# Routed experts offset by a pair: gate/up, a block of full-array products, then down of the preceding pair

## The chip, the cores and the metric

One core of a Trainium2 chip. The metric is the device time of one execution in microseconds (us). PE is TensorE, DVE is VectorE, ACT is ScalarE, POOL is GpSimd; SP is SyncE, whose queue issues the loads of the weights.

## What is computed

A network for 256 tokens of width 1024: two layers of a mixer and a routed feed-forward part with layer norms, and then two layers of three modulated sub-blocks each. The change lies in the routed experts of the first two layers:

```python
def routed_moe(x, router_w, router_b, w_gate, w_up, w_down):
    ...
    gates = ...          # for each token 2 of 16 experts, weights that sum to 1
    y = jnp.zeros_like(xt)
    for e in range(N_EXPERTS):
        h = jax.nn.silu(xt @ w_gate[e]) * (xt @ w_up[e])
        y = y + gates[:, e:e + 1] * (h @ w_down[e])
    return y.reshape(B, S, D)

ffn = routed_moe(x, ...)
x = layer_norm(ALPHA * x + ffn, ln_g[l, 1], ln_b[l, 1])
```

The inner width of an expert is 512, all of it in float32.

## The kernel before, in words

The program is a sequence of phases A to J. `in_weights` holds the weights of all phases in the order in which they are used, as loads of 1 MB, each of two chunks of 128 x 1024 numbers. SP issues the loads into a ring of blocks of 8 KB per partition (`NBLK = 23`, shared with the activations), as early as the plan of the blocks allows (`schedule`, `pump`, `raw`, L501). What the engines do is written as a program of tiles; a scheduler puts the instructions of each engine in order, so that a product which waits for something can stand behind later ones that are ready. All products go through `mm` (L587) and all transposes through `tr` (L591). An f32 product shows as two instructions of PE in the trace, one of type f32r as one.

Phases B and D (`phase_moe`, one for each of the first two layers) are the routed experts. Each expert takes its tokens in 64 slots. Two experts make a pair, eight pairs a phase, and the weights of a pair are 24 chunks: 16 of gate and up, 8 of down. `expert_pair` does for one pair:

- gate/up: per k-tile and expert two products of 64 columns with 512 numbers out, into `pg` and `pu`, one expert in the upper half of the partitions, the other in the lower half; 32 products. Then silu (ACT, L1352) and the product with up (DVE, L1353) make h.
- four transposes of h, copied by ACT (L1358) as hT.
- down: 16 products of 64 columns into two banks y; they leave y with the gate's factor and in two parts of type f32r, by ACT (L1379) and DVE (L1380).
- combine: eight products of all 128 columns with the transposed one-hot PT bring the slots back to the tokens; four additions into x by DVE (L1387).

Every second pair the slots of the next four experts are made: `onehot` (DVE, L1283), `gather` (32 products of 128 x 256, which leave by ACT, L1305, and DVE, L1302), and `slots` (transposes of the one-hots, and products that give the gates of the slots). After pair 5 `overflow` asks if an expert has more than 64 tokens: a branch on all engines (L1413, L1414). Its body does not run with these inputs. After it `gain_rows` makes sixteen transposes for the layer norm that follows. The last pair's combine goes into banks that hold x already, by products with the identity, and the layer norm takes it from there.

`behind` is a way to say that what is issued in it stands behind a given instruction in the order of its engine.

Of the kernel before, what the change touches and what calls it, by code (L numbers as in the profile page):

```python
# [18 lines left out]
D = 1024  # L19
# [7 lines left out]
# ---------------------------------------------------------------- host layout  # L27
# [27 lines left out]
# how many of the modulation's 144 columns of chunks are done by the end of a phase  # L55
# [13 lines left out]
def _mix_plan(p):  # L69
    """how many of its modulation chunks follow each of the main chunks of a phase"""  # L70
# [53 lines left out]
def _moe(inp, l):  # L124
    g, u, d = inp['moe_w_gate'][l], inp['moe_w_up'][l], inp['moe_w_down'][l]
    out = []
    for e in range(0, NE, 2):
# [149 lines left out]
def _consts():  # L277
# [18 lines left out]
    # of the attentions alone  # L296
# [44 lines left out]
class Null:  # L341
    """stands for any part of a program while its memory is planned"""
# [41 lines left out]
NW0, NW2 = 5, 2  # L384
# [3 lines left out]
class Net:  # L388
    NBLK = 23

    def __init__(self, ctx, tc, aps, phases, plan=None):
# [14 lines left out]
        self.nsplit, self.phase, self.last_mm = 0, None, []  # L406
# [5 lines left out]
    # ---- memory: blocks of 8 KB, for activations and for the weights that run ahead  # L412
# [19 lines left out]
    def free_up(self, u, lag):  # L432
        """the block is likely free `lag` weight chunks from now"""
# [8 lines left out]
    def schedule(self):  # L442
        """the event after which each weight load may be issued: as early as the blocks allow"""
# [45 lines left out]
    # ---- weight stream  # L489
# [57 lines left out]
    def splits_behind(self, *ins):  # L547
        """the next splits queue behind these instructions"""
# [12 lines left out]
    def behind(self, *ins):  # L561
        """what is issued here queues behind these instructions, each on its engine"""
# [6 lines left out]
    def sooner(self, n):  # L569
        """what is issued here goes before what came up to n instructions earlier, where either could"""  # L570
# [13 lines left out]
    # ---- matrix products  # L584

    def mm(self, out, a, b, start=True, stop=True):
        self.last_mm = [self.nc.tensor.matmul(out, lhsT=a, rhs=b, start=start, stop=stop)]  # L587
        return self.last_mm[0]

    def tr(self, out, a):  # L590
        self.nc.tensor.transpose(out, a, self.ident)  # L591
# [18 lines left out]
    def row(self, acc, x, first, last):  # L610
        """token-major product of one [128, 1024] slab; x = (hi, lo) [128, 256]"""
# [9 lines left out]
    def tail(self, acc, items, fin):  # L621
        """the last slabs of a token-major product, a piece of the output at a time; fin(t, n) follows piece n"""
# [13 lines left out]
    def hilo(self, src, hi, lo, eng=None):  # L636
        """exact parts of a tensor"""
# [3 lines left out]
    def feat_parts(self, x, t, scale, bias, hi, lo, act=False):  # L641
        """x [128 tok, 1024] of token tile t: x * scale + bias, feature-major, in parts"""
# [25 lines left out]
    def everywhere(self, a):  # L668
        """a vector of 1024, read once per partition"""
# [15 lines left out]
    # ---- constants  # L685

    def setup(self):
# [43 lines left out]
        self.onesb = cst.tile([128, 128], BF, name="onesb")  # L731
# [10 lines left out]
        self.modc = cst.tile([128, 2, 3, 24], F32, name="modc")  # L742
# [19 lines left out]
    def constants(self, *names):  # L762
        """a block with constants that only one phase needs"""
# [5 lines left out]
    # ---- norms  # L769
# [1540 lines left out]
```

## Time and profile before

| | |
|---|---|
| runs | 1987.99, 1991.94, 1994.36 us; median 1991.94 |
| the profiled execution | span 1988.0 us |
| PE | 95% busy, 11556 instructions |
| DVE | 60% |
| ACT | 44% |
| POOL | 24% |
| read from HBM | 504.00 MB, 254 GB/s over the span |
| granted clock of PE | 0.9 or more in each of 40 slices |

The span is that of the profiled execution, on the only core in use. PE's share over the span is a mean over phases with different limits, so the phases B and D are read by themselves: B from about 140 to 389 us, D from about 529 to 778 us. The granted clock 1.00 is 2.4 GHz, 0.50 is 1.2 GHz.

### The profile page before, as it was taken

Reading aid. Unit: us, or ns where it says so; the run is one execution under the profiler, and the core shown is the slowest. Engines: PE = TensorE matmul, PEld = TensorE weight load, DVE = VectorE, ACT = ScalarE, POOL = GpSimd, SP = SyncE. Lnnn points to the kernel's source line nnn. Section 1 sums busy time; section 2 is a strip of 40 time slices with the busy share of each in tenths; the row PEclk is TensorE's granted clock in tenths of the full one; section 3 lists DMA queues with packets and bytes.
Section 4 is the critical chain, followed back from the end, with each engine's and each line's share of the span. In section 5 each row is a group of like instructions: output and inputs, shape, how many; then the busy total and the mean of one; then the engine's idle time right before and its main releaser. Section 6 shows DMA issues by size and latency. Waiting matters only on the chain.

```text
span 1988.0 us, 29007 instructions
## 1 busy us (share of the span) xinstructions
PE 1885.5 (95%) x11556; PEld 1475.4 (74%) x11556; DVE 1186.6 (60%) x1951; ACT 878.2 (44%) x1522; POOL 475.8 (24%) x300
## 2 busy tenths in 40 slices
PE   7999998889999988999999899999989999999998
PEld 7874443377644434899898779998989888878997
DVE  6752221388421214989689978765977684567453
ACT  6631111166321112444597645455434566656443
POOL 2100000141000002343343332222431322354232
PEclk9999999999999999999999999999999999999999
DMA  9569999546799995787424558756786444555520
GB/s 388 208 242 358 406 421 371 217 151 232 296 354 419 421 387 238 299 336 275 180 90 176 210 213 317 299 189 249 277 336 236 170 149 147 193 212 212 195 103 33
DMA packets 70982, 507.08 MB, mean 255 GB/s; under 512 B 7856, under 2 KB 8112, under 8 KB 10032
## 3 DMA queue, kind: packets, MB, share of 16 engines
q1 hardware_dynamic: 70256, 503.15, 64.6%
q8 instruction: 94, 1.54, 0.3%
q10 hardware_dynamic: 576, 1.93, 0.2%
q14 instruction: 56, 0.46, 0.1%
HBM read 504.00 MB, written 1.05 MB: 254 GB/s over the span
## 4 chain that ended last, share of the span: by engine, by line
PE 47%; DVE 7%; ACT 4%; POOL 3%; issue 3%; DMA 0%; DVEq 0%; POOLq 0%; ACTq 0%
PE ph L587 27%; PE pg L587 19%; DVE t L580 2%; PE ph L591 1%; DVE t L539 1%; ACT t L579 1%; POOL t L580 1%; DMA t<-in_weights 0%; POOL w L2181 0%; ACT ph L844 0%; POOL t L2018 0%; DVE w L936 0%; DVE t L639 0%; DVE t L938 0%; POOL t L639 0%
## 5 line engine op out<-in xcount | busy, mean ns | idle before, releaser
L587 PE MATMUL pg<-t,t 128*128 128x512 f32 (+4 forms) x4702 | 974.1, 404 | 25.7 <-POOL t L580 9.1
L587 PEld LDWEIGHTS pg<-t,t 128*128 128x128 f32 (+1 forms) x4702 | 668.5, 180 | 244.6 <-issue 136.4
L587 PE MATMUL ph<-t,t 128*128 128x256 f32 (+3 forms) x4550 | 592.5, 290 | 7.1 <-ACT t L1615 3.1
L587 PEld LDWEIGHTS ph<-t,t 128*128 128x128 f32 (+2 forms) x4550 | 564.9, 192 | 25.0 <-ACT t L1615 4.1
L580 POOL TENSOR_TENSOR t<-t,t 128x1024 fp32r<-128x1024 f32 (+2 forms) x122 | 319.9, 2626 | 918.4 <-ACT t L579 809.3
L579 ACT ACTIVATE t<-t 128x1024 fp32r<-128x1024 f32 (+4 forms) x414 | 425.6, 1049 | 255.7 <-DVE t L580 60.6
L580 DVE TENSOR_TENSOR t<-t,t 128x1024 fp32r<-128x1024 f32 (+1 forms) x292 | 413.9, 1430 | 123.4 <-ACT t L579 120.8
L539 DVE SCALAR_TENSOR_TENSOR t<-t,cact 128x1024 f32<-128x1024 f32 x144 | 202.6, 1419 | 32.7 <-DMA t<-in_weights 32.5
L587 PE MATMUL ph<-t,w 128*64 128x512 f32 (+3 forms) x712 | 172.9, 546 | 7.6 <-ACT w L1358 6.0
L587 PEld LDWEIGHTS ph<-t,w 128*64 128x64 f32 (+1 forms) x712 | 70.4, 146 | 106.5 <-issue 71.4
L1353 DVE TENSOR_TENSOR w<-w,pg 128x512 f32<-128x512 f32 x16 | 11.0, 688 | 173.0 <-PE pg L587 129.4
L1380 DVE SCALAR_TENSOR_TENSOR t<-ph,rgsl,t 128x512 fp32r<-128x512 f32 x32 | 23.1, 748 | 150.1 <-ACT t L1379 149.9
L1352 ACT ACTIVATE w<-pg 128x512 f32<-128x512 f32 x16 | 9.6, 597 | 200.8 <-PE pg L587 200.8
L639 DVE TENSOR_TENSOR t<-w,t 128x256 fp32r<-128x256 f32 x96 | 79.9, 832 | 21.3 <-ACT t L638 21.2
L638 ACT ACTIVATE t<-w 128x256 fp32r<-128x256 f32 x107 | 43.6, 409 | 97.1 <-DVE w L1756 84.8
L1379 ACT ACTIVATE t<-ph,rgsl 128x512 fp32r<-128x512 f32 x32 | 20.9, 685 | 121.8 <-PE ph L587 121.3
L1756 DVE TENSOR_TENSOR w<-w,ph 128x256 f32<-128x256 f32 x88 | 36.6, 416 | 52.4 <-PE ph L587 50.6
L591 PE MATMUL ph<-kc,t 128*128 128x128 f32 x248 | 39.2, 284 | 25.0 <-DVE t L890 11.0
L1552 POOL MEMSET t<- 64x256 f32 x2 | 0.6, 306 | 250.8 <-PEq L1414 191.3
L1755 ACT ACTIVATE w<-ph 128x256 f32<-128x256 f32 x88 | 32.8, 372 | 51.3 <-PE ph L587 44.5
L587 PEld LDWEIGHTS ph<-w,t 128*128 128x128 f32 (+1 forms) x384 | 40.5, 171 | 18.1 <-issue 11.9
L591 PEld LDWEIGHTS ph<-kc,t 128*128 128x128 f32 x248 | 28.3, 143 | 33.8 <-issue 16.1
(334 smaller groups left out, 1408.8 us busy)
## 6 DMA issues: line engine op xcount, KB each, us to landing
t<-in_weights SPq DMA_DIRECT2D x475, 1024.0 KB, 7.5
t<-in_xT SPq DMA_DIRECT2D x2, 512.0 KB, 5.1
t<-in_weights SPq DMA_DIRECT2D x2, 512.0 KB, 6.5
t<-in_x SPq DMA_DIRECT2D x1, 1024.0 KB, 13.3
t<-in_gate_cols ACTq DMA_DIRECT2D x1, 864.0 KB, 7.0
t<-in_consts_attn SPq DMA_DIRECT2D x1, 512.0 KB, 3.5
t<-in_final_g ACTq DMA_DIRECT2D x1, 512.0 KB, 3.3
out<-t SPq DMA_DIRECT2D x2, 256.0 KB, 2.0
```

The costliest lines, as they stand in the source:

```text
L539: self.nc.vector.scalar_tensor_tensor(w, w, 1.0, self.cact, op0=OP.mult, op1=OP.mult, accum_out=acc)
L579: self.nc.scalar.activation(t[:, 0, :n], w[:, :n], AF.Copy)
L580: eng.tensor_tensor(t[:, 1, :n], w[:, :n], t[:, 0, :n].bitcast(F32), op=OP.subtract)
L587: self.last_mm = [self.nc.tensor.matmul(out, lhsT=a, rhs=b, start=start, stop=stop)]
L591: self.nc.tensor.transpose(out, a, self.ident)
L638: self.nc.scalar.activation(hi, src, AF.Copy)
L639: (eng or self.nc.vector).tensor_tensor(lo, src, hi.bitcast(F32), op=OP.subtract)
L1353: v.tensor_tensor(h, h, pu, op=OP.mult)
L1379: self.evac = nc.scalar.activation(yy[:, 0, ns], y[n], AF.Copy, scale=gsl[:, pr, :])
L1380: v.scalar_tensor_tensor(yy[:, 1, ns], y[n], gsl[:, pr, :], yy[:, 0, ns].bitcast(F32), op0=OP.mult, op1=OP.subtract)
L1755: nc.scalar.activation(a, g, AF.Silu)
L1756: nc.vector.tensor_tensor(a, a, u, op=OP.mult)
```

## The change

The pairs are offset by one. Step s does gate/up of pair s, then a block of the full-array products that are ready (the transposes of pair s - 1, gather and slots of the next four experts, combine of pair s - 2), then down of pair s - 1. The stream of weights has that order too. `pinned` puts each of the three behind the last instruction that PE was given, so that the scheduler doesn't mix them. The branch of the overflow stands after gate/up of pair 5, `gain_rows` in the block of step 6. Around it `NW0` (buffers of small tiles) goes from 5 to 6, the modulation's columns are changed in place and `modc` is gone, a matrix of ones becomes a column that is broadcast, a statistics tile shrinks, and comments are removed. In the changed kernel the lines are: `mm` L596, `tr` L601, silu L1359, its product L1360, hT L1368, y leaves by L1387 (ACT) and L1388 (DVE), additions into x L1413, the branch L1420 and L1421.

```diff
 def _moe(inp, l):
...
+    def gate_up(e):
...
+    def down(e):
...
+    gate_up(0)
+    for e in range(2, NE, 2):
+        gate_up(e)
+        down(e - 2)
+    down(NE - 2)
     return out
...
-NW0, NW2 = 5, 2
+NW0, NW2 = 6, 2
...
     def mm(self, out, a, b, start=True, stop=True):
         self.last_mm = [self.nc.tensor.matmul(out, lhsT=a, rhs=b, start=start, stop=stop)]
+        self.last_pe = self.last_mm[0]
         return self.last_mm[0]
...
-        def expert_pair(pr, xg, PT, gsl, nextw, fin=None, step=None, slots=None):
+        def gate_up(pr, xg, nextw, h, step=None):
...
-            PT = PT or slots()
-            h = self.w2([128, 512])
             nc.scalar.activation(h, pg, AF.Silu)
             v.tensor_tensor(h, h, pu, op=OP.mult)
+            return h
+
+        def turn(h, hT):
...
+        def down(pr, hT, gsl, nextw, then):
...
-            def combine(n):
+            def leave(n):
                 ns = PIECES[0][n]
                 self.evac = nc.scalar.activation(yy[:, 0, ns], y[n], AF.Copy, scale=gsl[:, pr, :])
                 v.scalar_tensor_tensor(yy[:, 1, ns], y[n], gsl[:, pr, :], yy[:, 0, ns].bitcast(F32),
                                        op0=OP.mult, op1=OP.subtract)
...
+                then(n, yy)
...
+        def combine(pr, yy, PT, n, c=None):
...
+        def pinned():
+
+            return self.behind(*[self.last_pe] * (self.last_pe is not None))
...
-        for p2 in range(4):
-            for pr in (2 * p2, 2 * p2 + 1):
-                PT = expert_pair(pr, cur[0][1], cur[1], gsl, stream, last if pr == 7 else None, None if pr else step,
-                                 lambda: slots(0, P, gsl, new))
-                cur = cur[0], PT
-                if pr % 2 == 0 and p2 < 3:
-                    nxt = pick(p2 + 1)
-            if p2 == 2:
-                overflow(cur[0])
...
+        for s in range(8):
+            p2 = s // 2
+            if s % 2 and p2 < 3:
+                P = onehot(p2 + 1, new)
+            with pinned():
+                hs[s] = gate_up(s, xg, stream, self.w2([128, 512]), None if s else step)
+            if s == 5:
+                overflow((ug, xg))
+                self.last_pe = None
+            if s % 2:
+                self.release(ug)
+            with pinned():
+                if s:
+                    hT = turn(hs.pop(s - 1), self.w2([128, 4, 128]))
+                else:
+                    PT[0] = slots(0, P, gsl, new)
+                if s % 2 and p2 < 3:
+                    ug, xg, _ = gather(P)
+                    PT[p2 + 1] = slots(p2 + 1, P, gsl, new)
+                if s == 5:
+                    self.release(*us)
+                if s > 1:
+                    uy, yy = ys.pop(s - 2)
+                    for n in range(2):
+                        combine(s - 2, yy, PT[s // 2 - 1], n)
+                    self.release(uy)
+                if s == 6:
+                    self.gb = self.gain_rows(l, 1)
...
+            if s:
+                with pinned():
+                    ys[s - 1] = down(s - 1, hT, gsl, stream, later)
...
+        with pinned():
+            h = hs.pop(7)
+            hT = turn(h, self.w2([128, 4, 128]))
+            c = {}
+            for t in range(2):
+                for n, ns in enumerate(PIECES[t]):
+                    c[t, n] = self.pg()
+                    self.mm(c[t, n], self.ident, x[:, t, ns], True, False)
+            uy, yy = ys.pop(6)
+            for n in range(2):
+                combine(6, yy, PT[3], n, c)
+            self.release(uy)
+        with pinned():
+            uy, _ = down(7, hT, gsl, stream, lambda n, yy: combine(7, yy, PT[3], n, c))
```

The order on PE before, in phase B around the end of a pair's down: `ph` with 64 rows is y of down, `ph` with 128 rows is combine, `pg` is gate/up of the next pair (one row is one product).

```order
L587 MATMUL ph_2124<-t_1956,w_393_2121 64x512
L587 MATMUL ph_2125<-t_1956,w_393_2121 64x512
L587 MATMUL pg_2174<-t_1956,t_1996 64x512
L587 MATMUL ph_2152<-t_2123,w_315_1771 128x512
L587 MATMUL ph_2156<-t_2123,w_315_1771 128x512
L587 MATMUL pg_2175<-t_1956,t_1996 64x512
L587 MATMUL ph_2152<-t_2123,w_315_1771 128x512
L587 MATMUL ph_2156<-t_2123,w_315_1771 128x512
L587 MATMUL ph_2162<-t_2123,w_315_1771 128x512 x2
L587 MATMUL ph_2166<-t_2123,w_315_1771 128x512 x2
L587 MATMUL pg_2174<-t_1962,t_1996 64x512
```

The same place on PE with the change: the end of gate/up, the block of a step of an even number (four transposes, combine), and the begin of down.

```order
L596 MATMUL pg_2102<-t_1960,t_1985 64x512
L596 MATMUL pg_2103<-t_1960,t_1985 64x512
L601 MATMUL ph_2155<-kc,w_350_1925 128x128 x4
L596 MATMUL ph_2161<-t_2070,w_312_1766 128x512 x2
L596 MATMUL ph_2165<-t_2070,w_312_1766 128x512 x2
L596 MATMUL ph_2169<-t_2070,w_312_1766 128x512 x2
L596 MATMUL ph_2173<-t_2070,w_312_1766 128x512 x2
L596 MATMUL ph_2178<-t_1960,w_400_2154 64x512
L596 MATMUL ph_2179<-t_1960,w_400_2154 64x512
L596 MATMUL ph_2178<-t_1966,w_400_2154 64x512
```

Combine now stands as one piece between the two runs of 64-column products, and its y is that of the pair before the one whose h is turned ahead of it.

The order on DVE before, in phase B for one pair: the product of silu and up (L1353), the second half of y's two pieces (L1380), the four additions into x (L1387).

```order
L1353 TENSOR_TENSOR w_391_2113<-w_391_2113,pg_2066 128x512
L1380 SCALAR_TENSOR_TENSOR t_2123<-ph_2124,rgsl_1510,t_2123 128x512
L1380 SCALAR_TENSOR_TENSOR t_2123<-ph_2125,rgsl_1510,t_2123 128x512
L1387 TENSOR_TENSOR t_67<-t_67,ph_2152 128x512
L1387 TENSOR_TENSOR t_67<-t_67,ph_2156 128x512
L1387 TENSOR_TENSOR t_67<-t_67,ph_2162 128x512
L1387 TENSOR_TENSOR t_67<-t_67,ph_2166 128x512
```

The same on DVE with the change, in a step of an even number.

```order
L1360 TENSOR_TENSOR w_389_2101<-w_389_2101,pg_2103 128x512
L1413 TENSOR_TENSOR t_67<-t_67,ph_2161 128x512
L1413 TENSOR_TENSOR t_67<-t_67,ph_2165 128x512
L1413 TENSOR_TENSOR t_67<-t_67,ph_2169 128x512
L1413 TENSOR_TENSOR t_67<-t_67,ph_2173 128x512
L1388 SCALAR_TENSOR_TENSOR t_2177<-ph_2178,rgsl_1509,t_2177 128x512
L1388 SCALAR_TENSOR_TENSOR t_2177<-ph_2179,rgsl_1509,t_2177 128x512
```

The additions of one pair now stand directly behind the product of silu and up of a later pair, and ahead of the evacuation of y of the pair between them.

## Rows read from the trace of the kernel before

**Rows 1.** The head of the page: span and instructions.

```profile
span 1988.0 us, 29007 instructions
```

**Rows 2.** Windows: busy time of each engine (instructions), PE's granted clock, DMA share, GB/s.

```profile
core 0: us, PE busy (x) PEld busy (x) DVE busy (x) ACT busy (x) POOL busy (x), PEclk, DMA share, GB/s
139.60:388.70 249.10, 235.98 (x1049) 101.95 (x1049) 50.68 (x96) 36.82 (x64) 1.62 (x5) 0.99 0.89 361
205.00:313.00 108.00, 103.21 (x476) 44.90 (x476) 22.87 (x44) 14.73 (x26) 0.00 (x0) 1.00 1.01 418
324.30:331.00 6.70, 5.93 (x22) 4.07 (x24) 0.00 (x0) 2.39 (x4) 0.61 (x2) 0.50 0.67 230
```

**Rows 3.** Waits of PE in B, 139 to 389 us: total, times, longest.

```profile
PE ph L591 <- DVE w L1353: 4.7, 5, 1.4
PE ph L591 <- DVEq L1414: 3.7, 1, 3.7
PE ph L587 <- ACT w L1358: 3.0, 4, 0.7
PE pg L587 <- ACT t L1379: 0.8, 1, 0.8
PE ph L587 <- ACT t L1379: 0.8, 1, 0.8
```

**Rows 4.** Waits of SP in the same stretch, its largest group.

```profile
SPq L501 <- PE ph L587: 75.7, 29, 6.6
```

**Rows 5.** DMA issues from 205 to 313 us: count, KB each, median us to landing.

```profile
t<-in_weights SPq DMA_DIRECT2D x45, 1024.0 KB, 15.9
```

**Rows 6.** Timeline of PE, 149 to 179 us: start, duration, instruction, count.

```profile
149.67 7.14 PE L587 MATMUL pg<-t,t 128*64 128x512 f32 x32
156.74 0.44 PE L591 MATMUL ph<-kc,w 128*128 128x128 f32 x2
...
158.08 1.07 PE L587 MATMUL pg<-t,t 128*64 128x512 f32 x2
159.08 0.66 PE L591 MATMUL ph<-kc,w 128*128 128x128 f32 x4
...
170.98 1.66 PE L587 MATMUL ph<-t,w 128*128 128x512 f32 x6
172.48 1.12 PE L587 MATMUL ph<-w,t 128*128 128x256 f32 x8
173.52 1.93 PE L587 MATMUL pg<-t,t 128*64 128x512 f32 x6
175.38 3.07 PE L587 MATMUL ph<-w,t 128*128 128x256 f32 x24
178.30 0.38 PE L591 MATMUL ph<-kc,w 128*128 128x128 f32 x2
```

**Rows 7.** Timeline of PE's weight loads in one run: first and last of 13.

```profile
194.49 0.15 PEld L587 LDWEIGHTS ph<-t,w 128*64 128x64 f32 x2 [0.28 <-issue]
...
199.64 0.15 PEld L587 LDWEIGHTS ph<-t,w 128*64 128x64 f32 x2 [0.28 <-issue]
```

**Rows 8.** Timeline of PE: behind the overflow's branch, and products by the identity.

```profile
325.07 3.65 PE L591 MATMUL ph<-kc,cols 128*128 128x128 f32 x16 [3.75 <-DVEq L1414]
...
359.64 1.98 PE L587 MATMUL pg<-t,kc 128*128 128x512 f32 x4
```

**Rows 9.** Timeline of PE: last down and end of B; begin and end of D.

```profile
376.08 4.51 PE L587 MATMUL ph<-t,w 128*64 128x512 f32 x18
...
388.69 2.35 PE L591 MATMUL ph<-kc 128*128 128x128 f32 x20
...
547.41 1.07 PE L587 MATMUL pg<-t,t 128*64 128x512 f32 x2
...
777.85 5.62 PE L591 MATMUL ph<-kc 128*128 128x128 f32 x50
```

**Rows 10.** The additions into x on DVE, over the span: shortest/median/longest ns.

```profile
L1387 DVE TENSOR_TENSOR t<-t,ph x56: 679/682/690, 171.5 to 747.7; 128x512 f32<-128x512 f32 x56
```

More of the change, by code (lines that the diff above doesn't have):

```diff
@@ L774, in normed @@
         nc, v = self.nc, self.nc.vector
-        st = self.small("lnst", [128, 2, 3, 6])
+        st = self.small("lnst", [128, 2, 2, 6])
         mv = self.small("lnmv", [128, 2, 2])
@@ L855, in prep @@
         v = self.nc.vector
-        c = self.modc[:, l, s, :]
-        v.tensor_tensor(c[:, :16], self.mod[:, l, s, :16], self.col(f'ab{l}{s}', 0, 16), op=OP.add)
+        c = self.mod[:, l, s, :]
+        v.tensor_tensor(c[:, :16], c[:, :16], self.col(f'ab{l}{s}', 0, 16), op=OP.add)
         v.scalar_tensor_tensor(c[:, 8:16], c[:, 8:16], 1.0, self.col(f'ng{l}{s}', 0, 8), op0=OP.add, op1=OP.mult)
@@ L862, in prep_gate @@
         v = self.nc.vector
-        c = self.modc[:, l, s, 16:]
-        v.tensor_tensor(c, self.mod[:, l, s, 16:], self.col(f'ab{l}{s}', 16, 8), op=OP.add)
+        c = self.mod[:, l, s, 16:]
+        v.tensor_tensor(c, c, self.col(f'ab{l}{s}', 16, 8), op=OP.add)
         v.tensor_scalar(c, c, 1.0, 1.0 if s == 1 else 0.5, op0=OP.add, op1=OP.mult)
@@ L873, in enter @@
         ul, lo = self.alloc([128, 8, S], F32R)
-        c = self.modc[:, l, s, :]
+        c = self.mod[:, l, s, :]
         uxs, xs = self.alloc([128, 2, 1024])
@@ L1356, in expert_pair, with some @@
                 self.tr(pt[:, k, :], h[:, k * 128:(k + 1) * 128])
-            hT = self.w2([128, 4, 128])
             nc.scalar.activation(hT, pt, AF.Copy)
+            return hT
+        def down(pr, hT, gsl, nextw, then):
             uy, yy = self.alloc([128, 2, 1024], F32R)
-            c = {}
-            if fin:
-                for t in range(2):
-                    for n, ns in enumerate(PIECES[t]):
-                        c[t, n] = self.pg()
-                        self.mm(c[t, n], self.ident, x[:, t, ns], True, False)
             y = [self.ph(), self.ph()]
-            def down(parts):
+            def some(parts):
                 for s in range(2):
@@ L1381, in combine @@
                                        op0=OP.mult, op1=OP.subtract)
-                for t in range(2):
-                    o = c[t, n] if fin else self.ph()
-                    for j in range(2):
-                        self.mm(o, PT[pr % 2][:, t * 128:(t + 1) * 128], yy[:, j, ns], j == 0 and not fin, j == 1)
-                    if not fin:
-                        v.tensor_tensor(x[:, t, ns], x[:, t, ns], o, op=OP.add)
+                then(n, yy)
             if pr == 7:
                 for n in range(2):
-                    down(((n, 0), (n, 1)))
-                    down(((n, 2), (n, 3)))
-                    combine(n)
+                    some(((n, 0), (n, 1)))
+                    some(((n, 2), (n, 3)))
+                    leave(n)
             else:
                 for k in range(4):
-                    down(((0, k), (1, k)))
+                    some(((0, k), (1, k)))
                 for n in range(2):
-                    combine(n)
-            fin_ = fin(h) if fin else None
-            for t, n in c:
-                with self.sooner(TAIL_AHEAD):
-                    fin_(t, n, c[t, n])
-            if fin:
-                self.release(self.gb[0])
-            self.release(uy)
-            return PT
+                    leave(n)
+            return uy, yy
+        def combine(pr, yy, PT, n, c=None):
+            ns = PIECES[0][n]
+            for t in range(2):
+                o = c[t, n] if c else self.ph()
+                for j in range(2):
+                    self.mm(o, PT[pr % 2][:, t * 128:(t + 1) * 128], yy[:, j, ns], j == 0 and not c,
+                            j == 1 and (pr == 7 or not c))
+                if not c:
+                    v.tensor_tensor(x[:, t, ns], x[:, t, ns], o, op=OP.add)
         base = self.pos
@@ L1440, in stream @@
             return (lambda: self.done(i)), w
-        def last(h):
-            self.release(*us)
-            self.warm(AF.Sqrt, h)
-            if l == 1:
-                self.prep(0, 0)
-            return self.normed(x, None, self.following(), self.gb[1])
         def new():
             return self.w0(F32R)
-        def pick(p2):
-            P = onehot(p2, new)
-            return gather(P)[:2], slots(p2, P, gsl, new)
         def affine():
@@ L1495, in begin_C @@
+        with pinned():
+            uy, _ = down(7, hT, gsl, stream, lambda n, yy: combine(7, yy, PT[3], n, c))
+        self.warm(AF.Sqrt, h)
+        if l == 1:
+            self.prep(0, 0)
+        fin = self.normed(x, None, self.following(), self.gb[1])
+        for t, n in c:
+            with self.sooner(TAIL_AHEAD):
+                fin(t, n, c[t, n])
+        self.release(self.gb[0])
+        self.release(uy)
     def begin_C(self):
```

51 lines of the change are left out of this document (28 added, 23 removed).

## Prediction

> **What bounds the kernel now.** I read the span first: 1988.0 us [rows 1]. The runs have a median of 1991.94 us, 3.9 us (0.2%) more; the sum below is made against the profiled execution and the 3.9 us are added at the end. A measurement of this kernel tells a change from none at about 0.3%, 6 us.
>
> Then the windows. In B, the first of the two phases that the change touches, PE is busy for 235.98 of 249.10 us at a granted clock of 0.99 [rows 2]; DVE has 50.68 us of work there and ACT 36.82. So PE sets the time, and what can be saved is in how long its products take, in its 13 us of idleness, or in nothing.
>
> The waits of PE in that stretch are few and none is on a DMA [rows 3]: 4.7 us for the silu's product (DVE, L1353) ahead of the transposes, 3.0 us for the copy of the transposed h (ACT, L1358) ahead of down, 0.8 us twice for the evacuation of y (ACT, L1379), and 3.7 us at the overflow's branch. In the other direction SP, which issues the weight loads, waits 75.7 us for PE in the largest of its groups alone [rows 4]: the weights wait for the products. But the stream has not much in reserve: from 205 to 313 us it moves 418 GB/s with the DMA engines' share at 1.01 [rows 2], which is 1.0486 MB / 418 GB/s = 2.51 us per load, and a load lands 15.9 us (median) after its issue [rows 5].
>
> Last, the timeline of PE, which shows what the products cost. There are two kinds: the weights' products use 64 columns of the array (128*64 in a row) and the others all of it (128*128). One f32 product of the weights is two instructions of the trace. In a long run two instructions come every 0.429 us (194.49 to 199.64 is 12 steps) [rows 7], and a run of 32 takes 156.74 - 149.67 = 7.07 us [rows 6]. Where such products stand between others they cost more: two alone take 159.08 - 158.08 = 1.00 us, six take 175.38 - 173.52 = 1.86 us [rows 6], against 0.43 and 1.29 by the pace of a long run. So each time PE goes from one kind to the other and back it loses 0.57 us, whatever it waits for. The place in PE's order of instructions shown with the change has four such passages in ten rows: one product of gate/up stands alone among those of combine.
>
> **The change, part by part.** Per phase I rebuild the whole from the end of the first slots (158.08 in B, 547.41 in D [rows 6, 9]) to the begin of the next phase's transposes (388.69 and 777.85 [rows 9]): 230.6 us and 230.4 us now. Later PE has the order that the rows of the change show: gate/up of pair s, a block of full-array products, down of pair s - 1, directly followed by gate/up of s + 1.
>
> *Runs.* Gate/up of a pair is 64 instructions, down 32. The first gate/up: 7.07 + 16 x 0.429 = 13.9 us. Then six runs of down and gate/up together, 96 instructions each: 7.07 + 32 x 0.429 = 20.8 us, 124.8 in all. Then down of pair 6 alone, 7.1 us. Sum 145.8 us. Whether a run goes on at this pace when it passes from down to gate/up is taken from the rows, where 0.429 holds for either.
>
> *Blocks.* Four transposes of h (the turn): 0.6 us [rows 6]. Combine, eight products: six take 172.48 - 170.98 = 1.50 us, so 2.0. Gather, 32 products: 24 take 178.30 - 175.38 = 2.92 us, so 3.9. Slots: 158.08 - 156.74 = 1.34 us. Blocks 1 to 7 are then turn, gather and slots 5.8; turn and combine 2.6; all four 7.8; 2.6; 7.8; turn, combine and the 16 transposes of the gain rows 4.5 (those are 3.65 us at half clock now [rows 8], 1.8 at full); 2.6. Sum 33.7.
>
> *Waits that go.* The turn of pair s - 1 stands behind gate/up of pair s, 13.9 us after its h is begun: the 4.7 us for L1353 go. The copy hT has the rest of the block to hide it: the 3.0 us go where combine or gather stands behind the turn, which is every block. Combine comes a whole step after its y: one 0.8 us goes; that of the last pair stays.
>
> *A wait that comes.* Down needs two banks for y and DVE frees them by the adds of combine, which stand in its order behind the product of the gate/up that has just ended (the place that I show on DVE). That product now ends 0.9 (mean) to 1.4 us behind PE [rows 3], and an add is 0.68 us [rows 10]. Two adds later is 2.3 to 2.8 us behind the end of gate/up; a block without gather lasts 2.6 us. Nothing if it runs smoothly, and if all four adds have to be done, 1.4 + 4 x 0.68 - 2.6 = 1.5 us. I take 0.5, since two banks are wanted and not four, in the four blocks without gather: 2.0 us. Behind DVE wait the two evacuations of down, which have the whole next gate/up to be done in.
>
> *The overflow's branch.* It stays, between gate/up 5 and block 5. PE waits there 3.75 us and its clock is 0.50 for the 6.7 us behind [rows 2, 8], which costs half of that, 3.4. I keep 4.4 (a few tenths more, as DVE has the product ahead of it) + 3.4 = 7.8 us.
>
> *The tail.* Turn of pair 7, four products of x by the identity, two of which (four instructions) take 1.98 us now [rows 8], and combine of pair 6: 0.6 + 3.9 + 2.0 = 6.5 us. Down of pair 7 with its combine keeps its order: 388.69 - 376.08 = 12.6 us [rows 9].
>
> *The rest at nothing.* NW0 from 5 to 6, modc in place, the column of ones and the smaller statistics tile move memory only; the other phases keep PE's order but for some rows of C's attention. If one of those edits cost a wait, it would be some tenths.
>
> Sum: 145.8 + 33.7 + 2.0 + 7.8 + 6.5 + 12.6 = 208.4 us, against 230.6 and 230.4: 22.2 + 22.0 = **44.2 us** less. 1988.0 - 44.2 + 3.9 = **1947.7 us**. From the other side: waits of 4.7 + 3.0 + 0.8 = 8.5 us less 2.0 new ones make 6.5 of the 22; the other 16 would be 28 passages there and back at 0.57 us, or 3.5 per pair. The sum's own bounds: the new wait from 0 to 1.5 (+-4 to 8 us over both phases), the tail and the branch some 2 us each way per phase: 1938 to 1958.
>
> **Does the stream keep up?** This is the step that I trust least. A load takes one of 23 blocks, some 15 loads are ahead. PE eats 12 loads per pair, in 28.8 us now (230.6 / 8), 2.4 us a load: a load is issued 36 us before its use and lands 20 us before it [rows 5]. Later a pair takes 20.8 and 5.5 (the mean block with its wait), 26.3 us, while 12 loads take 12 x 2.51 = 30.1. So 3.8 us of the 20 go per pair, 23 over six, and the branch gives 7.8 back: about 5 us are left at the end of the phase. My forecast is that PE waits for no weights, by a small margin.
>
> A rule speaks against even this margin. The Trainium skill, "DMA: Bandwidth & Descriptors", section "Where 436 GB/s comes from", says that transfers between HBM and SBUF are held by the HBM side, at about 358 GB/s per core; by it an estimate of 96 loads is 281 us per phase, and there would be no gain. The 418 GB/s over 108 us [rows 2] are above that figure, so here the measurement decides.
>
> **The rivals.**
>
> 1. *The weights become the bound.* If the stream gave not 418 but the 361 GB/s that B shows as its mean [rows 2], 12 loads would take 34.9 us, 8.6 more than a pair: over six pairs 52 us, less 28 of reserve and branch, 24 us of waits, and nothing saved: 1992. Against it: that mean holds times in which SP waited for PE; for it: the share of 1.01 says that no more comes. Halfway, 11 us per phase, is what I give it: **1969**. The sign would be waits of PE on in_weights in pairs 4 to 7. Chance 0.12.
> 2. *DVE sets the block.* Every block with a combine waits for all four adds and for the gather's evacuations in the same queue, 1.0 to 1.5 us more in six blocks of each phase, 12 to 18 us: **1962**. For it: DVE's order in the rows; against it: two banks suffice. Chance 0.06.
> 3. *More than the sum.* The new wait is nothing and the branch's 4.4 us of waiting too, 2 x (2.0 + 4.4) = 12.8 us: **1935**. Chance 0.03.
> 4. *Slower: PE's clock.* The block is pinned, so nothing fills a wait any more, where now the gate/up of the next pair does. One wait of 3.75 us is followed by 6.7 us at a granted clock of 0.50 [rows 2, 8], 7.2 us in all. At all 14 blocks that is some 100 us on top of the forecast: **2048**. It decides from 44.2 / 7.2, more than 6 of the 14 blocks. What could wait so long is down behind adds, evacuation and hT in one chain; the longest waits on DVE and ACT now are 1.4 and 0.8 us [rows 3], and behind those no clock falls (0.99 for the phase). Chance 0.03.
>
> That the change doesn't do what it says is excluded by the rows of the order; that its gain is eaten exactly, 0.01.
>
> **How the numbers follow.** The forecast has 0.75, rivals 1 to 4 0.12, 0.06, 0.03 and 0.03. Faster by over 0.3% are the forecast, rivals 2 and 3 and nine tenths of rival 1: 0.94. Within 0.3%: the end of rival 1 and the exact loss, 0.03; slower 0.03. The range takes 1938 to 1958 and reaches to rivals 2 and 3 and the nearer part of rival 1: 1935 to 1966.
>
> **What would show it.** Right: runs of 96 tiled instructions in some 20.8 us, no two of them alone between others; blocks of 3 to 8 us; no wait on L1353's successor; waits of about half a microsecond ahead of down on DVE; none on in_weights; next phase's transposes at about 366 in B. Wrong: waits on in_weights (rival 1), waits over 1 us ahead of down (2), a granted clock of 0.5 at the blocks (4). If the runs take more than 0.429 us per two instructions, the pace is not what I read from the rows.

## The result, and the profile after

The changed kernel takes 1939.1 us (median of 4 runs, 1938.25 to 1942.45), the kernel before beside it 1991.3: ratio 0.974, 95% interval [0.9726, 0.9754]. That is 52.2 us less where 44.2 were forecast, and inside the range. The head of the page of the changed kernel:

```profile
span 1937.2 us, 29029 instructions
```

Where the 50.8 us between the two spans went is read from PE's timeline, with the same landmarks as [rows 6, 9]: a phase's stretch runs from the first transposes of its first slots to the first transposes of the next phase. For D, which [rows 6, 9] show only in part, these are the begin before, and the begin and the end after:

```profile
546.07 0.44 PE L591 MATMUL ph<-kc,w 128*128 128x128 f32 x2
```

```profile
519.49 0.44 PE L601 MATMUL ph<-kc,w 128*128 128x128 f32 x2
...
727.46 5.62 PE L601 MATMUL ph<-kc 128*128 128x128 f32 x50
```

| us | before | after | difference |
|---|---|---|---|
| up to the slots of B | 156.74 | 158.37 | +1.6 |
| B | 231.95 | 207.49 | -24.5 |
| between (C) | 157.38 | 153.63 | -3.7 |
| D | 231.78 | 207.97 | -23.8 |
| the rest | 1210.2 | 1209.7 | -0.4 |

So the two phases of the change give 48.3 us, and C, which was not changed, 3.7. The small edits around it (`NW0`, `modc`, the column of ones) were not tried by themselves.

The timeline of PE after, in B: the first run, a block with gather, a run of 96 in two rows, a block with combine, the branch, and the end.

```profile
158.37 0.44 PE L601 MATMUL ph<-kc,w 128*128 128x128 f32 x2
...
159.71 14.00 PE L596 MATMUL pg<-t,t 128*64 128x512 f32 x64
173.65 0.66 PE L601 MATMUL ph<-kc,w 128*128 128x128 f32 x4
...
179.38 7.14 PE L596 MATMUL ph<-t,w 128*64 128x512 f32 x32
186.30 13.96 PE L596 MATMUL pg<-t,t 128*64 128x512 f32 x64
200.18 0.66 PE L601 MATMUL ph<-kc,w 128*128 128x128 f32 x4
200.59 9.39 PE L596 MATMUL ph<-t,w 128*128 128x512 f32 x40
...
261.75 13.96 PE L596 MATMUL pg<-t,t 128*64 128x512 f32 x64
282.65 1.09 PE L601 MATMUL ph<-kc,w 128*128 128x128 f32 x4 [6.94 <-DVEq L1421]
...
347.39 0.66 PE L601 MATMUL ph<-kc,w 128*128 128x128 f32 x4
...
353.26 4.50 PE L596 MATMUL ph<-t,w 128*64 128x512 f32 x18
...
365.85 2.34 PE L601 MATMUL ph<-kc 128*128 128x128 f32 x20
```

The run of 96 takes 200.18 - 179.38 = 20.80 us, the first gate/up 173.65 - 159.71 = 13.94, the block with gather 179.38 - 173.65 = 5.73. (A row of 40 instructions `ph` is combine, 8, and down, 32: both write `ph`.) Counted from the timeline, a phase had 36 runs of 64-column products, 20 of them with an odd number of products, and has 16, 2 of them odd.

The waits of PE in B, which answer to [rows 3], and of SP, which answer to [rows 4]:

```profile
PE ph L601 <- DVEq L1421: 6.9, 1, 6.9
PE pg L596 <- ACT t L1387: 0.8, 1, 0.8
```

```profile
SPq L510 <- DMA t<-in_weights: 76.4, 40, 3.0
SPq L510 <- PE pg L596: 48.0, 30, 4.7
...
SPq L510 <- PE ph L596: 38.2, 23, 6.7
```

The 4.7 us for silu's product and the 3.0 for hT are gone, no wait for in_weights has come, and the wait at the branch is 6.9 in place of 3.7. The largest group of SP's waits is now for its own transfers, 76.4 us where it was 16.0; its waits for PE fell from 148.5 to 86.2. The windows show the stream from 205 to 313 us at the pace of [rows 2], with the branch in it, and the clock behind the branch at half (0.50, 1.2 GHz):

```profile
205.00:313.00 108.00, 101.06 (x504) 55.48 (x500) 21.47 (x41) 14.95 (x27) 0.00 (x0) 0.97 1.01 420
```

```profile
282.65:285.50 2.85, 2.85 (x14) 2.85 (x15) 0.00 (x0) 1.16 (x2) 0.00 (x0) 0.50 1.00 417
```

### The profile page after: what moved, and what is told of

It is laid out like the page before. It is cut to its first block, busy times and chain, and to the rows that moved or that the text cites. A ratio compares the mean times of both kernels' runs of the same rounds, so it can differ in the third digit from the quotient of the medians.

```text
span 1937.2 us, 29029 instructions
## 1 busy us (share of the span) xinstructions
PE 1848.0 (95%) x11556; PEld 1495.1 (77%) x11556; DVE 1182.0 (61%) x1943; ACT 876.6 (45%) x1522; POOL 471.6 (24%) x300
## 4 chain that ended last, share of the span: by engine, by line
PE 49%; DVE 7%; ACT 4%; POOL 3%; issue 3%; DMA 1%; DVEq 0%; POOLq 0%; ACTq 0%
PE ph L596 29%; PE pg L596 19%; DVE t L589 2%; PE ph L601 1%; DVE t L548 1%; ACT t L588 1%; DMA t<-in_weights 1%; POOL t L589 1%; POOL w L2234 0%; DVE w L945 0%; ACT ph L853 0%; DVE t L899 0%; POOL t L2071 0%; DVE t L947 0%; POOL t L649 0%
## 5 line engine op out<-in xcount | busy, mean ns | idle before, releaser
L596 PE MATMUL pg<-t,t 128*128 128x512 f32 (+4 forms) x4702 | 941.5, 403 | 24.7 <-POOL t L589 9.3
L596 PEld LDWEIGHTS pg<-t,t 128*128 128x128 f32 (+1 forms) x4702 | 682.0, 181 | 227.7 <-issue 121.1
L596 PE MATMUL ph<-t,t 128*128 128x256 f32 (+3 forms) x4550 | 589.6, 289 | 7.6 <-ACT t L1668 3.8
L596 PEld LDWEIGHTS ph<-t,t 128*128 128x128 f32 (+2 forms) x4550 | 562.8, 191 | 25.0 <-ACT t L1668 4.4
L548 DVE SCALAR_TENSOR_TENSOR t<-t,cact 128x1024 f32<-128x1024 f32 x144 | 206.9, 1447 | 30.9 <-DMA t<-in_weights 30.9
L596 PE MATMUL ph<-t,w 128*64 128x512 f32 (+3 forms) x696 | 162.5, 546 | 0.0
L596 PEld LDWEIGHTS ph<-t,w 128*64 128x64 f32 (+1 forms) x696 | 75.6, 145 | 67.6 <-issue 56.3
L1360 DVE TENSOR_TENSOR w<-w,pg 128x512 f32<-128x512 f32 x16 | 11.0, 688 | 161.4 <-ACT w L1359 161.4
L1359 ACT ACTIVATE w<-pg 128x512 f32<-128x512 f32 x16 | 9.6, 597 | 191.5 <-PE pg L596 191.5
L1388 DVE SCALAR_TENSOR_TENSOR t<-ph,rgsl,t 128x512 fp32r<-128x512 f32 x32 | 22.7, 747 | 118.2 <-ACT t L1387 118.2
L1387 ACT ACTIVATE t<-ph,rgsl 128x512 fp32r<-128x512 f32 x32 | 20.5, 684 | 137.2 <-PE ph L596 128.4
L601 PE MATMUL ph<-kc,t 128*128 128x128 f32 x248 | 39.6, 285 | 23.3 <-DVE t L899 10.4
L601 PE MATMUL ph<-kc,w 128*128 128x128 f32 x192 | 36.1, 289 | 18.2 <-DVEq L1421 13.9
L601 PEld LDWEIGHTS ph<-kc,t 128*128 128x128 f32 x248 | 28.7, 144 | 31.8 <-issue 12.3
```

The costliest lines, as they stand in the source:

```text
L548: self.nc.vector.scalar_tensor_tensor(w, w, 1.0, self.cact, op0=OP.mult, op1=OP.mult, accum_out=acc)
L601: self.last_pe = self.nc.tensor.transpose(out, a, self.ident)
L1360: v.tensor_tensor(h, h, pu, op=OP.mult)
L1387: self.evac = nc.scalar.activation(yy[:, 0, ns], y[n], AF.Copy, scale=gsl[:, pr, :])
L1388: v.scalar_tensor_tensor(yy[:, 1, ns], y[n], gsl[:, pr, :], yy[:, 0, ns].bitcast(F32), op0=OP.mult, op1=OP.subtract)
```

## The experiments

The theory after the result: PE's time in B and D is set by how its products are grouped; the waits that the offset hides come second. The rivals: the waits alone; or the pins are only insurance and the order comes from the program by itself. All kernels are variants of the changed one; each median stands against a kernel before of 1991.2 to 1992.8 us on the same chip. Stretches of B and D are measured as in the table above.

### Without the pins

```diff
-            return self.behind(*[self.last_pe] * (self.last_pe is not None))
+            return ExitStack()
```

> The changed kernel with its pins taken away (pinned() returns an empty context), so that the scheduler may mix the products again; loop and stream stay. PE's order then has in B up to the branch four more runs of 64-column products than with the pins, two of them single products. If the order of the program (offset, blocks) makes the gain and the pins are only insurance: 2 to 4 us more per kernel, 1941 to 1946 us. If the pins make the gain: back to 1975 to 1992 us.

Measured: 1976.0 us, ratio 0.992 [0.9905, 0.9939]. B takes 222.71 us and D 223.16, 15.2 each over the changed kernel; C takes 157.39, as in the kernel before. Up to the branch PE's order in B is nearly that of the changed kernel (8 runs against 5); behind it the scheduler mixes again. The timeline of this kernel in B behind the branch:

```profile
304.03 3.60 PE L596 MATMUL pg<-t,t 128*64 128x512 f32 x12
307.55 0.33 PE L601 MATMUL ph<-kc,w 128*128 128x128 f32 x1
307.81 1.94 PE L596 MATMUL pg<-t,t 128*64 128x512 f32 x8
309.69 0.55 PE L601 MATMUL ph<-kc,w 128*128 128x128 f32 x3
```

Four transposes, combine and the gain rows are cut up among the products of gate/up. B's stretch has 23 runs where the pinned kernel has 11. At the pace of a long run, 0.429 us for two instructions [rows 7], the runs of the changed kernel in B take 4.8 us more than their instructions alone; here it is 13.9, in the kernel before 19.6. Its waits (10 us in all, the branch's 7.4 among them) are those of the changed kernel within 3 us. The second expectation holds, at its edge: the pins are worth 37 us of the 52, in a kernel whose program has the order already. They are more than insurance.

### Pieces of combine back among gate/up, even and odd

The edit of the even kernel is shown first, then the two places at which the odd one calls `piece` one product later.

```diff
...
+                def piece(k):
+                    if k in (6, 8):
+                        with pinned():
+                            combine(s - 2, yy, PT[s // 2 - 1], 0, None, [(k - 6) // 2])
...
-                    for n in range(2):
-                        combine(s - 2, yy, PT[s // 2 - 1], n)
+                    combine(s - 2, yy, PT[s // 2 - 1], 1)
...
```

```diff
-                if step:
+                if step and pr == 0:
...
+                    if step and pr and s == 0:
+                        step(k + AHEAD)
...
```

> The changed kernel with two of the four pieces of combine moved out of each block into the run of gate/up (behind k-tiles 2 and 4): 2 more runs of 64-column products per step, 6 steps, 2 phases, 24 more in all; each run keeps a whole number of k-tiles. Theory as predicted (0.57 us for each way there and back): 24 x 0.57 = 13.7 more, 1953 us. New theory (a run or a group of the other products loses only some 0.17 us at its begin, and the 0.43 is for a 64-column product without a partner): 24 x 0.33 = 8, 1947 us. Waits alone made the gain: no change, 1939 us.

> As e2_even, the pieces one product later: between the gate and the up product of the k-tile's first expert. As many runs as e2_even, but of 29, 8 and 11 products in place of 28, 8 and 12. Theory as predicted (only the ways there and back count): as e2_even, 1953 us. New theory: the runs of 29 and 11 lose half a pair each, 0.86 per step, and the 8 between may lose another 0.86: 10 to 21 us over e2_even, 1957 to 1968 us. Waits alone: 1939 us.

Measured: even 1951.3 us, ratio 0.979 [0.9774, 0.9806]; odd 1955.3 us, 0.982 [0.9797, 0.9849]. The medians don't decide: 1951.3 lies between the 1947 and the 1953 of the two theories, 1955.3 between their 1953 and 1957, and the two intervals overlap. They do rule out that the waits alone made the gain (1939). So the prices are read from one step and from the stretches. The same step (down of pair 0, gate/up of pair 2) in both, even first:

```profile
181.60 7.14 PE L596 MATMUL ph<-t,w 128*64 128x512 f32 x32
188.51 5.37 PE L596 MATMUL pg<-t,t 128*64 128x512 f32 x24
193.81 0.73 PE L596 MATMUL ph<-t,w 128*128 128x512 f32 x2
194.48 3.70 PE L596 MATMUL pg<-t,t 128*64 128x512 f32 x16
198.11 0.73 PE L596 MATMUL ph<-t,w 128*128 128x512 f32 x2
198.77 5.42 PE L596 MATMUL pg<-t,t 128*64 128x512 f32 x24
204.13 0.66 PE L601 MATMUL ph<-kc,w 128*128 128x128 f32 x4
```

```profile
179.22 7.14 PE L596 MATMUL ph<-t,w 128*64 128x512 f32 x32
186.14 6.17 PE L596 MATMUL pg<-t,t 128*64 128x512 f32 x26
192.24 0.73 PE L596 MATMUL ph<-t,w 128*128 128x512 f32 x2
192.91 3.65 PE L596 MATMUL pg<-t,t 128*64 128x512 f32 x16
196.49 0.74 PE L596 MATMUL ph<-t,w 128*128 128x512 f32 x2
197.16 5.37 PE L596 MATMUL pg<-t,t 128*64 128x512 f32 x22
202.46 0.66 PE L601 MATMUL ph<-kc,w 128*128 128x128 f32 x4
```

Even: 204.13 - 181.60 = 22.53 us, less the 20.80 of the unbroken run and 4 products of combine at 0.25 (1.0): 0.73 for two ways, **0.36 for each way there and back**. Odd: 23.24, so 1.44 for two. The 0.71 more lie in two places: 26 instructions take 6.10 and 22 take 5.30, together 0.74 more than twice 24 (5.30 and 5.36). A product is two instructions, so the runs are of 13 and 11 products in place of 12 and 12: each odd run loses 0.37 us, and a single 64-column product costs as much as two. It is read here as a product that has no partner beside it in the other half of the columns. The 8 products between lose nothing. Stretch by stretch: B and D take 5.2 and 3.8 us more than the changed kernel with even pieces, 8.6 and 7.7 with odd ones, for 12 ways each (12 x 0.36 = 4.4, and 4.4 more for 12 odd runs); 0.57 a way would have been 6.8 for both. The count is not all: in the kernel before, an even run of 52 instructions takes 373.72 - 361.56 = 12.16 us, 1.0 more than the pace of a long run gives, so that the order within a run seems to count too. That was not tried. The Trainium skill, "TensorEngine Tiling (Array Packing)", section "Key Properties", says that a change of the tiling mode drains the engine, and that tiles run independently of each other; both go with what is seen here, and the price, 0.36 us there and back, is this trace's.

### Without the offset

```diff
...
-                if s:
-                    hT = turn(hs.pop(s - 1), self.w2([128, 4, 128]))
+                if s == 0:
+                    PT[0] = slots(0, P, gsl, new)
                 else:
-                    PT[0] = slots(0, P, gsl, new)
+                    uy, yy = ys.pop(s - 1)
+                    for n in range(2):
+                        combine(s - 1, yy, PT[(s - 1) // 2], n)
+                    self.release(uy)
+                hT = turn(hs.pop(s), self.w2([128, 4, 128]))
...
-                if s > 1:
-                    uy, yy = ys.pop(s - 2)
...
-            if s:
-                with pinned():
-                    ys[s - 1] = down(s - 1, hT, gsl, stream, later)
+            with pinned():
+                ys[s] = down(s, hT, gsl, stream, later)
...
```

> The changed kernel without the offset: gate/up of pair s, a block (combine of pair s - 1, transposes of h of pair s itself, gather and slots, gain rows), down of pair s; stream in the old order, pins kept. One block per pair as before, so as many runs. If the grouping makes the gain: only the wait for hT shows in pairs 0, 2 and 4, 0.75 each, less one block of four transposes that goes: 2 to 5 us more, 1941 to 1944 us. If the offset makes it: the waits for h and for hT come back at every pair, 8 x (0.9 + 0.75) x 2 = 26 us more, 1965 us.

Measured: 1956.9 us, ratio 0.982 [0.9808, 0.9841]: 18 us over the changed kernel, between the two expectations. B takes 216.71 us, D 213.35, 9.2 and 5.4 more, and C 2.5 more. The waits of PE in B in this kernel:

```profile
PE ph L594 <- DVEq L1419: 8.5, 1, 8.5
...
PE ph L594 <- ACT w L1366: 2.2, 3, 0.7
...
PE ph L599 <- DVE w L1358: 0.6, 1, 0.6
```

The waits for h and hT are near the ones expected, 3.0 us in B and not eight times 1.65. All waits of PE together are 4.5 us longer than in the changed kernel in B and 4.0 in D. What was not expected: behind the first two of them the clock falls in B (not in D), and the branch's wait in B is 8.5 (in D 6.9). The windows of the stretch behind them:

```profile
161.10:163.00 1.90, 1.90 (x6) 0.71 (x8) 0.00 (x0) 0.00 (x0) 0.00 (x0) 0.59 0.99 410
163.00:166.00 3.00, 3.00 (x12) 0.99 (x9) 0.00 (x0) 0.00 (x0) 0.00 (x0) 0.69 0.66 240
```

Down of pair 0, 6.92 us elsewhere, takes 169.71 - 161.10 = 8.61 us there, 1.7 more. Pins without the offset are 36 us of the 52, the offset without the pins 17, and both together 52: nearly the sum.

### Six blocks less for the weights

```diff
-SLACK = {'A': 5, 'B': 3, 'C': 7, 'D': 2,
+SLACK = {'A': 5, 'B': 9, 'C': 7, 'D': 8,
```

> The changed kernel with six blocks less for the weights that run ahead in B and D (SLACK from 3 to 9 and from 2 to 8). By the prediction's estimate some 5 us of reserve are left at the end of a phase; six loads less ahead are 6 x 2.4 = 14 us less, so PE would wait some 10 us per phase for in_weights: 1958 us. By the trace of the changed kernel, where the tightest load of B lands 16 us before its product: 2 us are left and PE waits for no load: 1937 to 1941 us.

Measured: 1940.5 us, ratio 0.975 [0.9735, 0.9768], no wait for in_weights; B 207.65 and D 207.87. The landing of each load is set against the begin of its first product; in the paused kernel further down this gives 0.04 us for the loads that PE is seen to wait for, so the loads are matched rightly. By it the tightest load of B lands 11.3 us ahead in the changed kernel and 8.5 here. (The 16 us of the expectation are not borne out by this.) Six loads of reserve would have been 14 us, more than there is; what went is 2.8. So by then the DMA's pace sets how far ahead the loads are, and no longer the number of blocks.

### The branch in the middle of gate/up, and the first gather in one piece

```diff
...
+            banks, ks = None, range(8)
+            if s == 5:
+                with pinned():
+                    banks, ks = gate_up(s, xg, stream, None, None, range(MID)), range(MID, 8)
+                overflow()
+                self.last_pe = None
+                self.tr(self.ph()[:, :128], self.ident)
             with pinned():
-                hs[s] = gate_up(s, xg, stream, self.w2([128, 512]), None if s else step)
-            if s == 5:
-                overflow((ug, xg))
-                self.last_pe = None
+                hs[s] = gate_up(s, xg, stream, self.w2([128, 512]), None if s else step, ks, banks)
```

What the cut leaves out of this edit lets `gate_up` do a part of its k-tiles, and gives the body of the overflow blocks and banks of its own.

> The changed kernel with the overflow's branch in the middle of gate/up of pair 5 (behind k-tile 5), with one transpose behind it that nobody reads, so that the scheduler keeps the rest of gate/up behind the branch. DVE and ACT are idle there, so that they branch some 8 us before PE does. Theory that the wait is the sum of DVE's product (it stands ahead of its branch) and 5.4 us until DVE goes on behind the branch: PE now waits for its own branch alone, some 2 us in place of 6.9, 2 x 5 less, 2 x 0.4 more for two more ways between the kinds: 1929 to 1932 us. Rival, that every branch costs PE its 6 us wherever it stands: 1939 to 1941 us.

```diff
-        def gather(P, some=8, room=None):
+        def gather(P, some=8, room=None, act=0):
...
-                if k % 2 and (some == 8 or k > GACT):
+                if k % 2 and k >= act and (some == 8 or k > GACT):
...
-        ug, xg, step = gather(P, AHEAD)
+        ug, xg, step = gather(P, 8, None, 8)
```

> The changed kernel with the whole first gather of a phase ahead of gate/up of pair 0, its banks emptied by ACT alone (now three of its eight parts stand ahead and five between the k-tiles). Five runs of 64-column products less per phase. Theory that such a run costs 0.36 and 0.43 for each half pair: 2 x (1.8 + 0.4) = 4 us less, 1935 us. As predicted, 0.57 each: 5.7 less, 1933 us. Rival, that gate/up 0 then waits for ACT (eight evacuations of 0.56 us, 4.5 us against 3.9 us of products): 1938 to 1941 us.

> e5_mid and e6_all_first together, to see if they add: 2 x 5 and 4 us less, 1925 to 1928 us; if the clock or the stream takes one of them back, 1931 us or more.

Measured: 1938.8 us (0.974 [0.9723, 0.9755]), 1937.4 (0.9735 [0.9719, 0.9752]) and both 1935.0 (0.973 [0.9709, 0.9744]). The first and the last miss what was expected of them (1929 to 1932, 1925 to 1928), and the branch in the middle comes out at the time of its rival. The gather in one piece gains 1.7 of the 4 us in the median, less than these runs can tell apart; the first slots of B begin at 155.78 in place of 158.37 us, and gate/up 0 waits for nothing. With the branch in the middle B falls to 203.0 us, by the 5 us expected, but D rises to 210.1. The waits of PE in D of that kernel:

```profile
PE pg L596 <- issue: 4.2, 1, 4.2
...
PE ph L601 <- PEq L1423: 1.7, 1, 1.7
```

The branch's own wait is 1.7 and not 6.9, so the rival is not the reason. Three instructions behind it PE stops for 4.2 us with nothing to wait for that the profile shows; B has no such stop.

### The stream paused ahead of the branch, and no branch at all

```diff
+            if s == 4:
+                self.hold = True
             if s % 2:
                 self.release(ug)
```

> The changed kernel with no weight load issued from the end of gate/up 4 to the branch, so that the DMA engines should run dry before the engines jump; the loads that are left out there come behind the branch. Theory that the engines wait at the branch for code which is loaded behind the weights: DVE goes on some 3 us after its branch as in the kernel before (there the DMA had run dry) and not 5.4, PE's wait falls from 6.9 to about 4.5, 5 us less in all, 1934 us. Rival, that the wait is of the branch itself: 6.9 stays, 1939 us. If the stream can't spare the pause, PE waits for in_weights behind the branch, 1945 us or more.

```diff
-            if s == 5:
-                overflow((ug, xg))
-                self.last_pe = None
```

> The changed kernel without the overflow: neither the question nor the body is there, slots past the first 64 of an expert would be left out (these inputs have none). It prices the branch: 6.9 us of waiting and some 1.4 at half clock per phase, 16 to 17 us less, 1922 us, if PE's time behind it stays as it is; if the stream, which has had 7 us at the branch to catch up, then becomes the bound, 1927 us or more and waits on in_weights.

> The pause of e10_quiet with the branch in the middle of gate/up and the whole first gather ahead (e9_best). In e9_best D lost what B gained, by a second stop of 4.2 us just behind the branch that waits for nothing but the next instructions. Theory that this is code loaded behind the weights too: with the DMA quiet both stops shrink to 1 or 2 us, 1926 to 1929 us. Rival, that the second stop has another cause: 1933 to 1935 us as e9_best.

Measured: 1944.4 us (0.976 [0.974, 0.9777]), 1923.2 (0.964 [0.9628, 0.9661]) and 1930.1 (0.968 [0.9664, 0.9699]). The branch costs 16 us, as worked out from its waits and the half clock (2 x (6.9 + 1.4) = 16.6). The pause by itself made the kernel 5 us slower in the median and not 5 faster; the intervals of the two ratios overlap. What the branch waits for is seen in the rows of the branch's line: how long PE's sequencer is in it, and when DVE branches and goes on (first and last of B and D). The changed kernel, then the paused one, then the kernel before:

```profile
L1421 PEldq COMPARE_BRANCH  x2: 5948/5950/5952, 271.8 to 633.2; - x2
...
L1421 DVEq COMPARE_BRANCH  x2: 72/72/72, 277.1 to 638.4; - x2
...
L1421 DVEq EVENT_SEMAPHORE  x2: 21/21/21, 282.5 to 644.0; - x2
```

```profile
L1421 PEldq COMPARE_BRANCH  x2: 3472/3480/3488, 270.7 to 637.2; - x2
...
L1421 DVEq COMPARE_BRANCH  x2: 72/72/72, 275.9 to 642.4; - x2
...
L1421 DVEq EVENT_SEMAPHORE  x2: 21/21/21, 278.8 to 645.3; - x2
```

```profile
L1414 DVEq COMPARE_BRANCH  x2: 72/72/72, 322.0 to 711.0; - x2
...
L1414 DVEq EVENT_SEMAPHORE  x2: 21/21/21, 324.9 to 714.2; - x2
```

From branch to going on DVE takes 5.4 us in the changed kernel, 2.9 in the paused one and 2.9 in the kernel before (in D 5.6, 2.9 and 3.2); PE's sequencer 5.95 and 3.48 in the first two. The DMA's share was 1.01 from 276 to 283 us in the first, 0.02 from 270 to 276 us in the second and 0.09 from 322 to 325 us in the third. The wait of PE falls from 6.9 to 4.4 us in B and 4.2 in D. The trace has the transfers of code as packets of DMA queues of the kind "instruction". In B of the changed kernel the sequencers of PE, ACT and DVE branch at 271.8, 276.3 and 277.1 us, and such packets begin at 275.3, 279.8 and 280.5, each 3.5 us later. In the paused kernel the branches are at 270.7, 275.2 and 275.9 us and the packets at 271.7, 276.2 and 277.0, 0.9 to 1.1 us later. (Which packet is for which engine is taken from their order.) The pause is too long for this kernel all the same, since it takes the stream's reserve. PE's timeline of the paused kernel in pair 7:

```profile
329.85 1.94 PE L596 MATMUL pg<-t,t 128*64 128x512 f32 x8 [0.20 <-DMA t<-in_weights]
332.34 1.94 PE L596 MATMUL pg<-t,t 128*64 128x512 f32 x8 [0.54 <-DMA t<-in_weights]
```

This is what rival 1 would have looked like: a load every 2.49 us for products that take 1.72. With the branch in the middle and the first gather in one piece the same pause gains 5 us over that kernel without it: B 202.3 us, D 206.7, the second stop 1.7 us in place of 4.2. That kernel, at 1930.1 us (1926 to 1929 was expected), is the fastest of those that compute everything.

## Why the prediction was right, and where its steps were off

*The sum by steps.* Against 208.4 us from the end of the first slots the phases took 206.1 and 206.6. The runs came out as worked out (13.94 and 20.80 us). The blocks were some 1 us shorter: a turn between two groups is 0.41 us and not 0.6, because the row it was read from holds the way in and out. The wait for y's banks, taken as 0.5 in each of four blocks, doesn't show in the waits; three of the six runs behind a combine are 0.23 to 0.28 us longer than the others in B. The tail was 353.26 - 347.39 = 5.9, not 6.5. The branch was 6.9 of waiting and 1.4 at half clock, against 4.4 and 3.4. All of that is 4 of the 8 us by which the gain was larger.

*The other half lies outside the sum.* C, taken as unchanged, is 3.7 us shorter, and B begins 1.6 later. Its code is the same in all kernels of this study, but the scheduler's order of PE's products in C is not: the kernel before, the one without pins and the one without the offset share one order and take 156.2 to 157.4 us, and all others differ from it from PE's 347th instruction of C on and take 152.6 to 154.7. So the gain in C goes with a side effect on the scheduler's order; why that order is shorter was not tried. The rest is the difference of medians and spans: the medians lie 3.3 us over the profiled span before and 1.9 after, where I added 3.9.

*The step that failed in its mechanism* is the price of a change of kind: "each time PE goes from one kind to the other and back it loses 0.57 us, whatever it waits for". The runs show two prices: 0.36 for the way there and back, and 0.37 for a product without a partner. The rows had said so: two instructions cost 1.00 us [rows 6], and a run of four 1.01 in the same timeline, which I did not weigh:

```profile
139.59 1.08 PE L587 MATMUL pg<-t,t 128*64 128x512 f32 x4
140.60 0.61 PE L587 MATMUL ph<-w,t 128*128 128x256 f32 x3
```

The total didn't depend on this price. It rebuilds the phase at the pace of unbroken runs, which either price leaves as it is. Only the check "from the other side" uses it, with 28 ways at 0.57 for 16 us a phase. The timelines have 20 fewer runs and 18 fewer odd ones a phase, which at the two prices is 13.9 us, so that the agreement of the check was in part luck. Counted over B, the runs lost 14.8 us less over their instructions at the long run's pace (19.6 before, of which some 1.2 at half clock; 4.8 after), and PE's waits fell from 13.0 to 7.7 us. That is 20.1 of the 24.5 us of B, most of it by grouping.

*Does the stream keep up.* The sign was right, the reserve was mis-sized: "about 5 us are left at the end of the phase" against 11.3 at the tightest load. (The mean block with its wait is 35.7 / 7 = 5.1 us by my own terms, not 5.5; with it some 3 us would have been left.) I took 20 us for the reserve at the begin of the phase, but the first load of B lands 75 us ahead of its product, and that reserve is used up over the whole phase. The rule of the Trainium skill that the prediction cites ("DMA: Bandwidth & Descriptors", section "Where 436 GB/s comes from"), some 358 GB/s from HBM, did not hold here, with one core in use; 420 GB/s stood for 108 us.

*The rivals.* Rival 1 did not come, and was seen where the stream was paused. Rival 2 has one wait of 0.2 us on the gather's evacuation in D to show, and none in B. Of rival 3 one half came, a new wait near nothing; the branch's wait did not go but grew to 6.9. Rival 4 was nowhere near: no block but the one behind the branch has a wait ahead of it. I had put the gain down to order as a whole and not said that the pins carry most of it: the offset without them is worth a third.

## What to carry to other kernels

Where products of part of the array mix with those of all of it, count the changes of kind and the odd products in PE's order; here that was worth more than the waits that went (14.8 us against 5.3 in B). Writing the program in the wanted order isn't enough when a scheduler fills gaps: pin the groups, and look behind every branch in particular. Price a taken branch together with the DMA load around it, and check what a pause of the stream takes from its reserve before using one.

## What the runs showed of the hardware that was not expected

DVE goes on behind a taken branch 2.9 us later when the DMA engines are nearly idle (share 0.03 from 275.9 to 278.8 us in the paused kernel) and 5.4 us later when their share is 1.01. The Trainium skill, "Runtime: NRT & Kernel Launch", section "Instruction fetch mechanics", says that a taken branch whose target isn't at hand makes the engine fetch code by DMA before it goes on; the runs agree, with packets of the instruction queues between the branch and the going on, and add that these come 3.5 us behind a branch while the weights stream and 0.9 to 1.1 us behind it while they don't. The stop of 4.2 us shortly behind the branch, which fell to 1.7 with the stream paused, fits the next piece of code being fetched in the same way: in both kernels one packet of an instruction queue lies in the stop (from 630.9 us, and from 626.8 in the paused one), and PE goes on 1.4 us behind its end. That it waits for this packet is not shown beyond that, nor why B has no such stop. And the clock can fall in one phase and not in the other in the same place: without the offset, behind two waits of 0.6 and 0.7 us, the granted clock was 0.59 and 0.69 over 5 us in B, at the 1.2 GHz level for a part of them, while behind the same two waits in D it was 1.00 and left down of pair 0 at its full pace (540.89 - 533.97 = 6.92 us). Whether the waits made it fall is not shown.
